# The pooling mixer of a small decoder trunk as one listed order of single steps, with the rows around the tile borders pooled by one product

## Chip, cores and metric

One core of a Trainium2 chip runs the whole program in one launch. The metric is device time in microseconds (us) of a run; three runs of the kernel before gave 982.71 (median), 980.87 and 986.82. Everything else that is read here comes from one profiled execution.

## The reference

The input `x` holds 512 rows (positions) of 1024 channels. Layer 0 mixes by pooling, layer 1 by attention, and each layer ends in an MLP. What matters here is layer 0 up to the first half of its MLP, in 32-bit floats throughout:

```python
h = rms_norm(x, mix_pre_g[0])
# group g of 256 channels, window w = 2, 4, 8, 16: mean of the last w rows (fewer at the start), minus h itself
y[:, g] = causal_mean(h[:, g], w) - h[:, g]
m = (y[:, g] @ pool_w[0, g] for each g) * pool_scale[0]
x = x + rms_norm(m, mix_post_g[0])
h = rms_norm(x, mlp_pre_g[0])
x = x + rms_norm(square(relu(h @ w_up[0])) @ w_down[0], mlp_post_g[0])
```

`rms_norm(x, g)` is `x * (mean(x*x) + 1e-6) ** -0.5 * g`.

## The kernel before

The 512 rows are four tiles of 128 rows, `xt[0]` to `xt[3]`, kept on the chip. The stage that is changed runs from the start of the program to the second halves of the first up blocks. For each tile `t`, of which every product has two halves `h` of 512 channels, it does this:

- **Square** (`q`): ScalarE sums the squares of a row. **Norm** (`x`): VectorE adds the two parts of the sum and EPS, GpSimd takes the power -0.5 (`rstd`), VectorE multiplies the tile by it into `xs[t]`.
- **Pool** (`p`): TensorE multiplies 128x128 blocks of `xs[t]` by a constant band matrix (its columns hold the weights of a mean minus the identity), and for tiles 1 to 3 adds a second product of 16 columns with the tile before, `xs[t-1]`, since a window reaches back over the border. ScalarE copies the result, which stands channels by rows, to `ys[t]`.
- **Mix** (`m`): TensorE multiplies by the group's map `wpool` (already scaled on VectorE by `linear`, step `w`, with `mix_pre_g` and with `pool_scale`, which `spread`, step `r`, has spread over all partitions by a product of a one-row matrix of ones). ScalarE sums the squares of the result, VectorE multiplies it by the gain `mix_post_g`.
- **Add** (`a`): VectorE, GpSimd and VectorE again make the factor of that norm and add to `xt[t]`; ScalarE sums the squares of the new `xt[t]`.
- **Norm and transpose** (`n`, `t`): the same three-engine chain makes the next factor, VectorE multiplies into a tile `xn`, TensorE transposes it, and ScalarE and VectorE split it into a high and a low part, `xnh` and `xnl`.

The first matrix of the MLP is worked in blocks of 128 output columns. Each block is split into high and low too (`weight`: a load, a ScalarE cast, a VectorE subtraction; step `F` does the next block) and needs three products for each of eight channel blocks. An up block has a first half, tiles 0 and 1 (256 columns), and a second half, tiles 2 and 3; `u0` to `u3` are the first halves of blocks 0 to 3, done inside the mixing stage.

Steps named `z` are warm-up products of a tile of zeros into a bank that nobody reads; there are 20. PSUM gives eight banks, taken in turn. `MIX_ORDER` lists the steps, and inside `tc.manual_schedule` each engine runs its instructions in the order in which the steps issue them. The tiles 2 and 3 that are still to be transposed at the end of the list are done by the MLP code (`pending`, `need`). Loads are issued by SyncE in the order of the code, each waiting for the one eight places before it.

After the stage the MLP (`mlp`) does the four second halves, block 4 whole, and then products of groups of blocks (line 507) that need `w_down` rows, of which one half is loaded into the buffer `xn3` of the `xn` tiles.

In `Update.rstd` the row factor of the MLP norm is taken without EPS, and `homogeneous_eps` makes up for it later with three VectorE operations of one column for each tile and layer.

Of the kernel before, what the change touches and what calls it, by code (L numbers as in the profile page):

```python
# [15 lines left out]
P = 128  # L16
D = 1024
S = 512
# [13 lines left out]
TINY = 1e-24  # L32
# [12 lines left out]
    for w in """q0 z8 r z6 q1 x0 p00 p01 z6 x1 w0 p10 p11 w1 q2 m00 x2 q3 m01 a0 m10 m11 x3 p20 p21 n0  # L45
    p30 a1 t00 t01 p31 F n1 m20 m21 F t10 t11 u0 a2 m30 F m31 u1 n2 a3 F t20 t21 u2 n3 F u3""".split()
# [11 lines left out]


# [6 lines left out]
def trunk(ctx, tc, x, consts, gcol, grow, pw, wup, wdn, wq, wk, wv, wo, out):  # L66
# [20 lines left out]
    xt = [keep.tile([P, D], F32, tag=f"x{t}", name=f"x{t}") for t in range(T)]  # L87
# [160 lines left out]
    def rstd(st, col, eps=EPS, op=ALU.add, third=False):  # L248


        total = st[:, col + 2 : col + 3]
        latest["dve"] = nc.vector.tensor_scalar(
            out=total, in0=st[:, col : col + 1], scalar1=st[:, col + 1 : col + 2],
            scalar2=eps, op0=ALU.add, op1=op,
        )
# [3 lines left out]
        latest["pool"] = nc.gpsimd.tensor_tensor(out=r, in0=total, in1=mhalf, op=ALU.pow)  # L259
        return r  # L260
# [12 lines left out]
    mlp_eps, normed_by, early = {}, {}, []  # L273

    class Update:
        def __init__(self, t, gpost, scaled, eps=EPS, gpre=None, final=False):
            self.t, self.gpost, self.scaled, self.eps = t, gpost, scaled, eps
# [12 lines left out]
        def add(self):  # L290
            r = rstd(self.st, 0, self.eps, third=len(self.cuts) > 2)
            x = xt[self.t]
            for n, cut in enumerate(self.cuts):
                latest["dve"] = nc.vector.scalar_tensor_tensor(
                    out=x[:, cut], in0=self.scaled[:, cut], scalar=r, in1=x[:, cut], op0=ALU.mult, op1=ALU.add
                )
                if self.final:
                    nc.sync.dma_start(out[TS[self.t], cut], x[:, cut])
                else:
                    square_sum(x[:, cut], self.xn[:, cut], self.st, 4 + n)  # L300

        def rstd(self):
            normed_by[self.t] = self
            if self.gpre is None:
                self.r = rstd(self.st, 4)
                return

            self.r = rstd(self.st, 4, TINY, ALU.max)  # L310

        def homogeneous_eps(self):
            m, q, r = self.st[:, 6:7], self.st[:, 0:1], self.r
            e = mlp_eps[self.t] = keep.tile([P, 1], F32, tag=f"eps{self.t}", bufs=2, name=name("eps"))
            nc.vector.tensor_scalar(out=q, in0=m, scalar1=EPS, scalar2=r, op0=ALU.add, op1=ALU.mult)
            nc.vector.tensor_scalar(out=q, in0=q, scalar1=r, scalar2=None, op0=ALU.mult)
            nc.vector.scalar_tensor_tensor(out=e, in0=q, scalar=EPS, in1=q, op0=ALU.mult, op1=ALU.mult)
# [200 lines left out]
    def mlp(l, mp, update):  # L518
# [33 lines left out]
        entering = dict(normed_by)  # L552
# [22 lines left out]
        for g, group in enumerate(groups):  # L575
# [51 lines left out]
    with tc.tile_pool(name="mix0", bufs=1, reuse_waits="tile") as mp:  # L627
# [3 lines left out]
        cst = mp.tile([P, 12 * P], F32, tag="cst", name="cst")  # L631
        band = lambda kind, g: cst[:, (kind * 4 + g) * P : (kind * 4 + g + 1) * P]
        one_row = mp.tile([1, D], F32, tag="row", name="row")
        ones = mp.tile([1, P], F32, tag="ones", name="ones")
        nc.gpsimd.memset(ones, 1.0)
        nc.sync.dma_start(cst[:, : 4 * P], consts[:, P : 5 * P])
        nc.sync.dma_start(one_row, grow[R_SCALE : R_SCALE + 1, :])
        nc.sync.dma_start(gc, gcol)
        nc.sync.dma_start(xt[1], x[TS[1], :])
        wpool = [mp.tile([P, D], F32, tag=f"pw{i}", name=f"pw{i}") for i in range(2)]  # L640
        nc.sync.dma_start(cst[:, 4 * P :], consts[:, 5 * P :])
        for i in range(2):
            nc.sync.dma_start(wpool[i], pw[i])
        gpost = gain_row(R_MIX_POST0)
        nc.sync.dma_start(xt[2], x[TS[2], :])
        nc.sync.dma_start(xt[3], x[TS[3], :])
        nc.sync.dma_start(ident, consts[:, :P])
        gpre0 = gain_row(R_MLP_PRE0, spare_tile())

        scale = mp.tile([P, D], F32, tag="scale", name="scale")  # L650
        xs, ys, ups, sts = {}, {}, {}, {}
# [6 lines left out]
        def spread():  # L658

            for n in NS:  # L660
                pr = ps()
                nc.tensor.matmul(pr, ones, one_row[:, n], start=True, stop=True)
                nc.scalar.copy(scale[:, n], pr)

        def linear(i):


            for b in range(4):
                k, g = C_MIX_PRE0 * KC + 4 * i + b, 2 * i + b // 2
                w = wpool[i][:, b * 256 : (b + 1) * 256]  # L670
                nc.vector.scalar_tensor_tensor(
                    out=w, in0=w, scalar=gc[:, k : k + 1], in1=scale[:, g * 256 : (g + 1) * 256],
                    op0=ALU.mult, op1=ALU.mult,
                )

        def squares(t):
            xs[t] = mp.tile([P, D], F32, tag=f"xs{t}", name=f"xs{t}")
            sts[t] = keep.tile([P, 8], F32, tag=f"stat{t}", bufs=4, name=name("stat"))
            if t == 0:
                for n in range(2):  # L680
                    square_sum(xt[t][:, NS[n]], xs[t][:, NS[n]], sts[t], n)
            else:
                nc.vector.memset(sts[t][:, 1:2], 0.0)
                square_sum(xt[t], xs[t], sts[t], 0)

        def scaled(t):
            r = rstd(sts[t], 0)
            for n in NS:
                nc.vector.tensor_scalar(out=xs[t][:, n], in0=xt[t][:, n], scalar1=r, scalar2=None, op0=ALU.mult)

        def pooled(t, h):
            if not h:
                ys[t] = mp.tile([P, D], F32, tag="y", bufs=2, name=f"y{t}")
            py = ps()
            for c in range(4):
                cb = 4 * h + c
                cs = slice(cb * P, (cb + 1) * P)
                nc.tensor.matmul(
                    py[:, TS[c]], xs[t][:, cs], band(0 if t == 0 else 1, cb // 2), start=True, stop=True,
                    skip_group_check=True,  # L700
                )
                if t:

                    n = max(WINDOWS)
                    nc.tensor.matmul(
                        py[:, c * P : c * P + n], xs[t - 1][:, cs], band(2, cb // 2)[:, :n], start=False,
                        stop=True, skip_group_check=True,
                    )
            nc.scalar.copy(ys[t][:, NS[h]], py)

        def mixed(t, h):
            if not h:
                ups[t] = Update(t, gpost, mp.tile([P, D], F32, tag="m", bufs=2, name=f"m{t}"), gpre=gpre0)
            pm = ps()
            for g in (2 * h, 2 * h + 1):
                o = pm[:, (g % 2) * 256 : (g % 2) * 256 + 256]
                for k in range(2):
                    cs = slice((2 * g + k) * P, (2 * g + k + 1) * P)
                    ws = slice(((g % 2) * 2 + k) * 256, ((g % 2) * 2 + k) * 256 + 256)
                    nc.tensor.matmul(o, ys[t][:, cs], wpool[h][:, ws], start=k == 0, stop=k == 1)  # L720
            ups[t].square(h, pm, nc.vector)

        def normed(t):
            ups[t].rstd()
            ups[t].norm()
            pending[t] = ups[t]

        def transposed(t, h):
            ups[t].transpose((h,))
            if h:  # L730
                pending.pop(t)

        def half_up(j):
            early.append((ps(), get(("up", 0, j))))
            up_block(*early[j], slice(0, S // 2))

        steps = {
            "q": squares, "x": scaled, "p": pooled, "m": mixed, "a": lambda t: ups[t].add(), "n": normed,
            "t": transposed, "r": spread, "w": linear, "F": fill, "z": busy, "u": half_up,
        }  # L740
        on = mybir.EngineType
        with tc.manual_schedule(engines={on.PE, on.Activation, on.DVE, on.Pool}):
            for step, which in MIX_ORDER:
                steps[step](*which)


    with tc.tile_pool(name="mlp0", bufs=1, reuse_waits="tile") as mp:
        mlp(0, mp, lambda t, y, gpost: Update(t, gpost, y, mlp_eps[t]))
# [204 lines left out]
    with tc.tile_pool(name="mlp1", bufs=1, reuse_waits="tile") as mp:  # L953
        mlp(1, mp, lambda t, y, gpost: Update(t, gpost, y, mlp_eps[t], final=True))


def constants():
# [4 lines left out]
    first, later, before = [], [], []  # L962
    for w in WINDOWS:
        inside = ((s <= t) & (s > t - w)).astype(np.float32)
        first.append(inside / np.minimum(t + 1, w).astype(np.float32) - eye)
        later.append(inside / np.float32(w) - eye)
        before.append((s - P > t - w).astype(np.float32) / np.float32(w))
    return np.concatenate([eye, *first, *later, *before], axis=1).astype(np.float32)
# [38 lines left out]
```

## Time and profile before

| | before |
|---|---|
| runs, median (lowest to highest) | 982.71 us (980.87 to 986.82) |
| profiled execution: span from first to last instruction | 984.6 us |
| TensorE (PE) busy | 959.1 us, 97% |
| VectorE (DVE) busy | 715.6 us, 73% |
| ScalarE (ACT) busy | 566.9 us, 58% |
| GpSimd (POOL) busy | 138.5 us, 14% |
| DMA | 156.88 MB, mean 159 GB/s |

The profile has no time of the profiled execution besides its span; 984.6 us is 1.9 us above the median of the runs and inside their spread. PE is the engine of the matrix products, PEld its weight loads, SPq the queue of SyncE that issues loads. A timeline row gives start and duration in us, engine, line, operation, output<-input tiles, shape and count; where the engine was idle ahead of it, brackets give how long and what ended it. Tile names are shown without their numbers.

### The profile page before, as it was taken

To read this page: it belongs to the slowest core of one execution; us is meant where nothing else is said; L and a number is where in the kernel's file an instruction comes from. 1 tells how busy PE (TensorE), PEld (TensorE's weight loads), DVE (VectorE), ACT (ScalarE), POOL (GpSimd) and SP (SyncE) were. 2 spreads that over 40 slices of the span, in tenths; PEclk is the share of its full clock that TensorE was granted. 3 is DMA by queue.
4 is the path that set the end of the run, shared out by engine and by line. 5 is a ranking of instruction groups with operands and counts; after the bars stand their busy time and mean duration, and the time that the engine had idled before them with its cause. 6 is when DMAs were issued, how large, how long until landed. Compare 5 with 4: busy or idle time off the path is not lost.

```text
span 984.6 us, 12507 instructions
## 1 busy us (share of the span) xinstructions
PE 959.1 (97%) x4804; PEld 812.2 (82%) x4804; DVE 715.6 (73%) x772; ACT 566.9 (58%) x979; POOL 138.5 (14%) x107
## 2 busy tenths in 40 slices
PE   9799999999999999999999999989999999999997
PEld 6688888878788788999799987888888888888885
DVE  3647589897897986376667688775487785957856
ACT  4537888978695556465556573446454444444532
POOL 1102030130402204100000000302031210302103
PEclk9899999999999999999999999989999999999999
DMA  6153777959678690242352423243333314133012
GB/s 249 44 192 98 265 275 227 416 199 346 243 277 326 232 342 3 89 169 86 129 214 89 168 108 121 77 145 108 128 102 112 128 56 181 29 127 122 22 43 87
DMA packets 43550, 156.88 MB, mean 159 GB/s; under 512 B 4449, under 2 KB 4833, under 8 KB 43490
## 3 DMA queue, kind: packets, MB, share of 16 engines
q1 hardware_dynamic: 43490, 156.07, 44.4%
q8 instruction: 38, 0.62, 0.2%
q14 instruction: 22, 0.18, 0.1%
HBM read 122.50 MB, written 33.55 MB: 159 GB/s over the span
## 4 chain that ended last, share of the span: by engine, by line
PE 82%; DVE 8%; ACT 4%; issue 2%; DMA 2%; POOL 1%; POOLq 0%; DVEq 0%; ACTq 0%
PE ps L507 24%; PE ps L623 13%; PE ps L624 13%; PE ps L622 13%; PE ps L264 4%; PE ps L265 4%; PE ps L263 4%; DMA xn<-in_wdn 2%; PE ps L895 2%; DVE w L130 2%; PE ps L885 1%; DVE w L243 1%; PE ps L853 1%; PE ps L854 1%; ACT xn L246 1%
## 5 line engine op out<-in xcount | busy, mean ns | idle before, releaser
L507 PE MATMUL ps<-w,a 128*128 128x512 f32 x1176 | 278.4, 389 | 2.4 <-DVE a L243 2.4
L623 PE MATMUL ps<-xnl,w 128*128 128x512 f32 (+1 forms) x712 | 263.9, 371 | 1.9 <-DVE xnl L243 1.9
L624 PE MATMUL ps<-xnh,w 128*128 128x512 f32 (+1 forms) x712 | 263.5, 370 | 0.8 <-DVE w L130 0.8
L622 PE MATMUL ps<-xnh,w 128*128 128x512 f32 (+1 forms) x712 | 263.8, 372 | 0.4 <-ACT w L128 0.4
L507 PEld LDWEIGHTS ps<-w,a 128*128 128x128 f32 x1176 | 220.5, 188 | 49.4 <-DVE a L243 3.7
L623 PEld LDWEIGHTS ps<-xnl,w 128*128 128x128 f32 x712 | 136.3, 191 | 24.3 <-DVE xnl L243 2.5
L624 PEld LDWEIGHTS ps<-xnh,w 128*128 128x128 f32 x712 | 136.2, 191 | 23.2 <-DVE w L130 1.0
L622 PEld LDWEIGHTS ps<-xnh,w 128*128 128x128 f32 x712 | 135.8, 191 | 22.8 <-ACT w L128 0.6
L130 DVE TENSOR_TENSOR w<-raw,w 128x1024 fp32r<-128x1024 f32 x66 | 83.9, 1271 | 60.2 <-ACT w L128 60.2
L128 ACT CAST w<-raw 128x1024 fp32r<-128x1024 f32 x66 | 69.0, 1047 | 84.7 <-PE ps L624 79.0
L516 DVE TENSOR_TENSOR y<-ps,y 128x512 f32<-128x512 f32 x124 | 83.2, 683 | 34.9 <-PE ps L507 34.9
L242 ACT CAST a<-r 128x768 fp32r<-128x768 f32 (+1 forms) x60 | 47.6, 793 | 65.0 <-PE ps L507 39.4
L462 POOL TENSOR_TENSOR s<-r 128x768 f32<-128x768 f32 (+1 forms) x10 | 21.7, 2172 | 373.8 <-ACT r L540 331.2
L242 ACT CAST w<-e 128x1536 fp32r<-128x1536 f32 (+1 forms) x30 | 41.9, 1398 | 54.0 <-DVE e L481 44.7
L243 DVE TENSOR_TENSOR a<-r,a 128x768 fp32r<-128x768 f32 (+1 forms) x60 | 60.0, 1003 | 14.6 <-ACT a L242 14.5
L288 POOL TENSOR_TENSOR y<-y,grow 128x512 f32<-128x512 f32 x12 | 18.7, 1556 | 314.1 <-ACT xn L246 314.1
L243 DVE TENSOR_TENSOR w<-e,w 128x1536 fp32r<-128x1536 f32 (+1 forms) x30 | 58.3, 1943 | 4.5 <-ACT w L242 4.2
L462 POOL TENSOR_TENSOR r<-r 128x768 f32<-128x768 f32 (+1 forms) x20 | 48.7, 2437 | 64.5 <-DVE a L243 49.7
L867 DVE TENSOR_TENSOR_SCAN e<-u,begin 128x1280 f32<-128x1280 f32 x16 | 45.2, 2822 | 13.3 <-ACT u L861 13.0
L139 ACT ACTIVATE apart<-apart,gc 128x128 f32<-128x128 f32 (+1 forms) x132 | 42.8, 406 | 0.0
L246 ACT ACTIVATE xn<-y 128x512 f32<-128x512 f32 (+1 forms) x25 | 15.4, 616 | 41.8 <-DVE y L369 41.8
L243 DVE TENSOR_TENSOR w<-xn,w 128x1536 fp32r<-128x1536 f32 (+1 forms) x20 | 33.0, 1651 | 5.5 <-ACT w L242 5.5
(127 smaller groups left out, 1509.9 us busy)
## 6 DMA issues: line engine op xcount, KB each, us to landing
raw<-in_wup SPq DMA_DIRECT2D x62, 512.0 KB, 3.8
w<-kept SPq DMA_DIRECT2D x58, 512.0 KB, 4.2
kept<-wx SPq DMA_DIRECT2D x30, 512.0 KB, 5.2
w<-in_wdn SPq DMA_DIRECT2D x8, 1536.0 KB, 6.4
kept<-apart SPq DMA_DIRECT2D x24, 512.0 KB, 5.1
xn<-in_wdn SPq DMA_DIRECT2D x8, 1536.0 KB, 8.3
raw<-in_wdn SPq DMA_DIRECT2D x8, 512.0 KB, 4.3
apart<-in_wk SPq DMA_DIRECT2D x7, 512.0 KB, 8.8
```

Of the source, the lines that this page charges most:

```text
L128: nc.scalar.copy(hi, raw)
L130: nc.vector.tensor_tensor(out=lo, in0=raw, in1=hi.bitcast(F32), op=ALU.subtract)
L139: nc.scalar.mul(c, c, gc[:, lo + k : lo + k + 1])
L242: latest["act"] = nc.scalar.copy(hi, src)
L243: latest["dve"] = nc.vector.tensor_tensor(out=lo, in0=src, in1=hi.bitcast(F32), op=ALU.subtract)
L462: sub = lambda out, x, y, op=ALU.subtract: nc.gpsimd.tensor_tensor(out=out, in0=x, in1=y, op=op)
L507: nc.tensor.matmul(bank, a[:, x, q, TS[t]], w[:, z, q], start=start and q == 0 and k == 0, stop=q == self.n - 1 and k == 2, skip_group_che ...
L516: nc.vector.tensor_tensor(out=part, in0=bank, in1=part, op=ALU.add)
L622: nc.tensor.matmul(pu[:, cols], wh[:, k, :], xnh[:, k, cols], start=k == 0, stop=False)
L623: nc.tensor.matmul(pu[:, cols], wh[:, k, :], xnl[:, k, cols], start=False, stop=False)
L624: nc.tensor.matmul(pu[:, cols], wl[:, k, :], xnh[:, k, cols], start=False, stop=k == KC - 1)
L867: nc.vector.tensor_tensor_scan(out=e[:, ::-1], data0=u[:, 1:][:, ::-1], data1=begin[:, ::-1], initial=0.0, op0=ALU.mult, op1=ALU.max,)
```

## The change

The mixing stage becomes one list of 135 single steps, each of one engine (`h` issues its load too), and the list takes in what was left to the MLP code and to `fill`: all transposes, the splits of up weights 0 to 3 (`h`, `l`) and the four first halves (`U`).

- **The row norm moves into the band.** `x` isn't scaled any more. The sum of squares goes straight to GpSimd's power (the tiles are two columns wider, and the extra column holds the value whose square stands for EPS), and VectorE multiplies the constant band (`b`) by the row factor.
- **The borders are pooled by one product.** The 30 rows around each of the three borders are loaded once more into a tile `edge` (90 rows), and one set of products of 46 columns gives the 15 rows behind each border. The tiles 1 to 3 then need products of 114 columns for their other 113 rows, and none with the tile before.
- `spread` has matrices of 128 rows, all but one zero, in place of one row. Nine warm-up products are left of 20: eight ahead and one behind the two spreads. The loads stand in another order: the maps and the edge rows come ahead of `xt[1]`.
- The pooled rows of all tiles go to one tile `yt`. The additions to `xt` are one instruction of 1024 columns in place of two of 512, and so are the squares of the new `xt`.
- EPS is added in every norm, and `homogeneous_eps` with its 24 VectorE instructions is gone.

The core of the diff:

```diff
-    for w in """q0 z8 r z6 q1 x0 p00 p01 z6 x1 w0 p10 p11 w1 q2 m00 x2 q3 m01 a0 m10 m11 x3 p20 p21 n0
-    p30 a1 t00 t01 p31 F n1 m20 m21 F t10 t11 u0 a2 m30 F m31 u1 n2 a3 F t20 t21 u2 n3 F u3""".split()
+    for w in """z8 S0 q0 C0 S1 r0 b0 z1 P00 L00 L02 C1 c00 P01 L03 q4 L01 L13 r4 L10 L11 c01 L12 M00 M01 b4 q1 r1 b1 s00
...
-            self.r = rstd(self.st, 4, TINY, ALU.max)
-
-        def homogeneous_eps(self):
-            m, q, r = self.st[:, 6:7], self.st[:, 0:1], self.r
...
-            else:
-                with tc.issue_after(latest["dve"].ins):
-                    while entering:
-                        entering.popitem()[1].homogeneous_eps()
...
+        edge = mp.tile([3 * EDGE, D + 2], F32, tag="edge", name="edge")
+        windows = {**dict(enumerate(xt)), T: edge}
+        for w in windows.values():
+            nc.vector.memset(w[:, D:], (EPS * D) ** 0.5)
...
         for i in range(2):
             nc.sync.dma_start(wpool[i], pw[i])
+        for i in range(3):
+            lo = (i + 1) * P - EDGE // 2
+            nc.sync.dma_start(edge[i * EDGE : (i + 1) * EDGE, :D], x[lo : lo + EDGE, :])
+        nc.sync.dma_start(xt[1][:, :D], x[TS[1], :])
...
+        def mean_square(t, col):
+            r = rows(t)
+            nc.scalar.activation(
+                junk[r, : D + 1], windows[t][:, : D + 1], ACT.Square, scale=D**-0.5,
+                accum_out=sts[t][r, col : col + 1],
+            )
...
+        def power(t, col):
+            r = rows(t)
+            nc.gpsimd.tensor_tensor(
+                out=sts[t][r, col + 1 : col + 2], in0=sts[t][r, col : col + 1], in1=mhalf[r], op=ALU.pow
+            )
+
+        def scaled_band(t):
+            kind, r = 0 if t == 0 else 2 if t == T else 1, rows(t)
+            n = 4 * BANDS[kind]
+            band[t] = mp.tile([P, 4 * P], F32, tag="band", bufs=3, name=f"band{t}")
+            nc.vector.tensor_scalar(
+                out=band[t][r, :n], in0=bands[r, starts[kind] : starts[kind] + n], scalar1=sts[t][r, 1:2],
+                scalar2=None, op0=ALU.mult,
+            )
+
+        def pooled(t, h):
+            py = pys[t, h] = ps()
+            n, r = BANDS[0 if t == 0 else 2 if t == T else 1], rows(t)
+            at = BORDER if t == T else P
+            for i, c in enumerate(range(KC) if t == T else range(4 * h, 4 * h + 4)):
+                nc.tensor.matmul(
+                    py[:, i * at : i * at + n], windows[t][r, c * P : (c + 1) * P],
+                    band[t][r, c // 2 * n : c // 2 * n + n], start=True, stop=True, skip_group_check=True,
                 )
-                if t:
-
-                    n = max(WINDOWS)
-                    nc.tensor.matmul(
-                        py[:, c * P : c * P + n], xs[t - 1][:, cs], band(2, cb // 2)[:, :n], start=False,
-                        stop=True, skip_group_check=True,
-                    )
...
+        steps = {
+            "q": squares, "r": lambda t: power(t, 0), "b": scaled_band, "P": pooled, "c": pooled_out,
+            "S": spread, "C": spread_out, "L": linear, "M": mixed, "s": mixed_square, "g": mixed_gain,
+            "e": total, "E": lambda t: power(t, 4), "A": added, "w": lambda t: mean_square(t, 6),
+            "v": lambda t: power(t, 6), "N": normed, "T": transposed, "H": high, "X": low,
+            "h": weight_high, "l": weight_low, "U": half_up, "z": busy,
+        }
```

A step's digits are its tile and half (`T20`: tile 2, first half; tile 4 is `edge`), or its block (`U3`, `h3`, `l3`).

What the lists make of the engines' queues is seen in two places. On TensorE, where tile 2 is pooled out and the up blocks begin, the kernel before has this (L698 and L705 pool, L720 mixes, L334 transposes, L622 to L624 are the up block):

```order
L698 MATMUL ps25_306<-cst_88,xs3_213 128x128
L705 MATMUL ps25_306<-cst_88,xs2_196 128x16
L720 MATMUL ps29_327<-pw0_96,y2_250 128x256 x4
L720 MATMUL ps30_334<-pw1_97,y2_250 128x256 x4
L334 MATMUL ps33_346<-ident_74,xn3_80 128x128 x4
L334 MATMUL ps34_353<-ident_74,xn3_80 128x128 x4
L622 MATMUL ps35_360<-xnh_81,w26_316 128x256
```

and the changed one this (L708 pools, L731 mixes, L765 transposes, L607 to L609 are the up block):

```order
L765 MATMUL ps32_287<-ident_74,xn3_80 128x128 x4
L731 MATMUL ps33_292<-pw0_99,yt_120 128x256 x4
L731 MATMUL ps34_297<-pw1_100,yt_120 128x256 x4
L731 MATMUL ps35_308<-pw0_99,yt_120 128x256 x4
L765 MATMUL ps36_315<-ident_74,xn3_80 128x128 x4
L708 MATMUL ps38_322<-band2_206,x2_72 128x114 x4
L765 MATMUL ps39_329<-ident_74,xn3_80 128x128 x4
L731 MATMUL ps40_336<-pw1_100,yt_120 128x256 x4
L607 MATMUL ps41_348<-xnh_81,w23_247 128x256
```

Before, the first up block stands right behind the transposes of tile 1, with the mixes of tile 3 behind it; now all mixes stand ahead of the up blocks, and between the two transposes of tile 1 (ps36, ps39) stands a pooling product that doesn't need them.

On VectorE, the kernel before has this around the splits of tile 1 (L243 splits, L252 is the one-column sum ahead of GpSimd's power, L294 adds to `xt`, L288 applies the gain, L130 splits a weight, L325 norms):

```order
L130 TENSOR_TENSOR w31_341<-raw32_342,w31_341 128x1024
L243 TENSOR_TENSOR xnl_82<-ps33_346,xnh_81 128x4x128
L243 TENSOR_TENSOR xnl_82<-ps34_353,xnh_81 128x4x128
L252 TENSOR_SCALAR stat28_326<-stat28_326 128x1
L294 SCALAR_TENSOR_TENSOR x2_72<-m2_325,stat28_326,x2_72 128x512 x2
L288 TENSOR_TENSOR m3_391<-ps37_393,grow1_101 128x512
```

and the changed one this (L756 norms, L739 gain, L777 splits, L743 sum, L749 adds):

```order
L756 SCALAR_TENSOR_TENSOR xn3_80<-x1_71,stat12_179,spare2_116 128x512 x2
L739 TENSOR_TENSOR m37_320<-ps34_297,grow1_112 128x512
L777 TENSOR_TENSOR xnl_82<-ps32_287,xnh_81 128x4x128
L777 TENSOR_TENSOR xnl_82<-ps36_315,xnh_81 128x4x128
L777 TENSOR_TENSOR xnl_82<-ps39_329,xnh_81 128x4x128
L743 TENSOR_SCALAR stat17_214<-stat17_214 128x1
L739 TENSOR_TENSOR m37_320<-ps33_292,grow1_112 128x512
L749 SCALAR_TENSOR_TENSOR x3_73<-m37_320,stat17_214,x3_73 128x1024
```

The split of an up weight no longer stands right ahead of the splits of tile 1, and tile 3 is worked ahead of tile 2.

More of the change, by code (lines that the diff above doesn't have):

```diff
@@ L44 @@
     (w[0], [int(c) for c in w[1:]])
-    for w in """q0 z8 r z6 q1 x0 p00 p01 z6 x1 w0 p10 p11 w1 q2 m00 x2 q3 m01 a0 m10 m11 x3 p20 p21 n0
-    p30 a1 t00 t01 p31 F n1 m20 m21 F t10 t11 u0 a2 m30 F m31 u1 n2 a3 F t20 t21 u2 n3 F u3""".split()
+    for w in """z8 S0 q0 C0 S1 r0 b0 z1 P00 L00 L02 C1 c00 P01 L03 q4 L01 L13 r4 L10 L11 c01 L12 M00 M01 b4 q1 r1 b1 s00
+    q2 s01 g00 e0 r2 P40 c40 g01 E0 b2 A0 P10 q3 c10 P11 r3 w0 P20 b3 v0 c11 M10 N00 P30 N01 h0 M11 T00 P31
+    l0 s10 h1 c30 g10 s11 l1 c20 e1 g11 H00 E1 A1 X00 c31 h2 T01 M30 M31 w1 v1 l2 s30 N10 s31 M20 H01 N11 T10
+    g31 P21 X01 H10 T11 c21 H11 M21 s21 X10 X11 e3 s20 g30 E3 U0 A3 w3 g21 e2 g20 h3 E2 A2 w2 v3 U1 N30 N31
+    v2 l3 N21 T30 H30 U2 T21 T31 H31 N20 H21 T20 X30 X31 H20 X21 X20 U3""".split()
 ]
@@ L630, in trunk @@
         nc.gpsimd.memset(warm, 0.0)
[L631 to L634, printed above, removed]
+        row = mp.tile([P, D], F32, tag="row", name="row")
+        nc.vector.memset(row, 0.0)
+        ones = mp.tile([P, P], F32, tag="ones", name="ones")
         nc.gpsimd.memset(ones, 1.0)
-        nc.sync.dma_start(cst[:, : 4 * P], consts[:, P : 5 * P])
@@ L652, in trunk @@
+        yt = mp.tile([P, KC, S], F32, tag="yt", name="yt")
+        sts, band, pys, pms, ms, xns, pts, pus = {}, {}, {}, {}, {}, {}, {}, {}
         pwarm = ps()
@@ L676, in squares @@
[L676 to L689, printed above, removed]
@@ L961, in constants @@
     eye = (s == t).astype(np.float32)
-    first, later, before = [], [], []
+    first, rest, border = [], [], []
     for w in WINDOWS:
```

179 lines of the change are left out of this document (109 added, 70 removed).

## The prediction

> **What bounds the kernel now.** I read the page first: how long, and by what.
>
> ```profile
> span 984.6 us, 12507 instructions
> ...
> PE 82%; DVE 8%; ACT 4%; issue 2%; DMA 2%; POOL 1%; POOLq 0%; DVEq 0%; ACTq 0%
> ```
>
> TensorE makes 82% of the chain that ended last. The rest must stand somewhere, so I cut the start by the view of windows (columns: window, its length, PE busy, weight loads, DVE, ACT, POOL, granted clock, DMA share, GB/s). The chain of waits puts the first second half of an up block at 66.99 and the first product of line 507 at 84.47; the other cuts are where the clock changes.
>
> ```profile
> 1.31:66.99 65.68, 58.18 (x329) 46.73 (x329) 33.26 (x65) 29.09 (x64) 6.69 (x13) 0.95 0.43 158
> 43.35:50.17 6.82, 5.45 (x24) 5.41 (x25) 3.45 (x6) 1.39 (x4) 0.55 (x1) 0.50 0.26 80
> 50.17:66.99 16.82, 15.02 (x105) 13.25 (x103) 9.57 (x16) 6.19 (x13) 1.65 (x3) 1.00 0.54 187
> 66.99:84.47 17.48, 17.48 (x121) 16.33 (x122) 11.38 (x11) 10.21 (x15) 0.68 (x1) 1.00 0.47 155
> 84.47:130.00 45.53, 45.53 (x203) 37.70 (x202) 28.11 (x28) 36.76 (x64) 6.82 (x6) 1.00 0.63 217
> ```
>
> From 66.99 on PE has no gap: 17.48 of 17.48 and 45.53 of 45.53. So whatever makes PE reach that point earlier shifts the rest with it. In the changed stage PE is idle for 65.68 - 58.18 = 7.5 us, and runs a spell of 6.82 us at half the clock. Who it waits for:
>
> ```profile
> PE ps L334 <- DVE xn L325: 2.8, 2, 2.2
> PE ps L623 <- DVE xnl L243: 1.9, 1, 1.9
> PE ps L698 <- DVE xs L689: 1.4, 1, 1.4
> ```
>
> These 6.1 of the 7.5 us are VectorE's results arriving late: norm, split and scaling, in a queue where each stands behind another tile's work.
>
> **The prices.** From the timeline, the step from one row's start to the next:
>
> ```profile
> 1.31 3.60 PE L656 MATMUL ps<-warm 128*128 128x512 bf16 x8 [1.31 <-POOL warm L630]
> ...
> 4.29 0.63 ACT L246 ACTIVATE xs<-x 128x512 f32<-128x512 f32 x1
> ...
> 4.84 3.78 PE L662 MATMUL ps<-row,ones 1*128 1x512 f32 x4
> 8.55 2.74 PE L656 MATMUL ps<-warm 128*128 128x512 bf16 x6
> 11.09 2.69 PE L698 MATMUL ps<-cst,xs 128*128 128x128 f32 x16
> 13.61 1.46 PE L656 MATMUL ps<-warm 128*128 128x512 bf16 x6
> ...
> 15.27 0.47 PE L698 MATMUL ps<-cst,xs 128*128 128x128 f32 x2
> 15.57 0.29 PE L705 MATMUL ps<-cst,xs 128*128 128x16 f32 x2
> 15.71 0.47 PE L698 MATMUL ps<-cst,xs 128*128 128x128 f32 x2
> ...
> 18.39 7.15 PE L720 MATMUL ps<-pw,y 128*128 128x256 f32 x32
> 25.38 0.39 PE L698 MATMUL ps<-cst,xs 128*128 128x128 f32 x2
> ...
> 32.31 1.33 PE L334 MATMUL ps<-ident,xn 128*128 128x128 f32 x8
> 33.48 0.39 PE L698 MATMUL ps<-cst,xs 128*128 128x128 f32 x2
> ...
> 45.53 0.41 PE L623 MATMUL ps<-xnl,w 128*128 128x256 f32 x1
> 45.74 0.41 PE L624 MATMUL ps<-xnh,w 128*128 128x256 f32 x1
> ...
> 56.07 0.28 PE L623 MATMUL ps<-xnl,w 128*128 128x256 f32 x1
> 56.19 0.28 PE L624 MATMUL ps<-xnh,w 128*128 128x256 f32 x1
> ```
>
> - Warm-up product: (11.09 - 8.55)/6 = 0.42 us early, about 0.22 us in the row of 13.61. So the clock was half until some point behind 11.09 and full before 13.61.
> - Both spreads: 8.55 - 4.84 = 3.71.
> - Pooling: a block of 128 columns with its border product is four rows, 15.71 - 15.27 = 0.44; 0.11 a row, whether of 128 columns or of 16. A half tile of four blocks: 1.76 with borders, 0.88 without. (Two rows are one 32-bit product.)
> - A mix: (25.38 - 18.39)/32 x 8 = 1.75. A half tile's transposes: (33.48 - 32.31)/2 = 0.58.
> - A first half of an up block is 24 products: at 0.12 each 2.88; in the half-clock spell at 0.21 it is 5.1, so that spell cost block 0 about 2.2.
>
> Products of 46 and 114 columns don't occur before. Below, 0.11 a row times 46/128 is 0.04; above, 0.11. I take 0.11, since 16 columns cost as much as 128 there. P40 is then 16 x 0.11 = 1.76, or 0.64 at the least.
>
> **PE's sum.** Before, work at these prices: warm-ups 14 x 0.42 + 6 x 0.22 = 7.2, spreads 3.7, pooling of tile 0 2.5 (11.09 to 13.61), of the others 6 x 1.76 = 10.6, mixes 14.0, transposes 4.7, up halves 11.5 + 2.2. That is 56.4 of 65.68, so 9.3 are waits with their filling and draining. After: nine warm-ups 8 x 0.42 + 0.22 = 3.6, spreads 3.7, pooling 8 x 0.88 + 1.76 = 8.8, mixes 14.0, transposes 4.7, up halves 11.5: 46.3. With 0.2 for the row that the spreads read, PE would be through at 1.31 + 46.5 = 47.8 if it never waited.
>
> **What PE waits for after.** I walked the four listed queues with the durations of these groups (mean ns), ends of one engine to starts of the next 0.05 us apart.
>
> ```profile
> L246 ACT ACTIVATE xs<-x 128x1024 f32<-128x1024 f32 x3 | 3.2, 1056 | 0.0
> L246 ACT ACTIVATE xn<-ps 128x512 f32<-128x512 f32 x8 | 4.8, 597 | 4.0 <-PE ps L720 3.8
> L259 POOL TENSOR_TENSOR stat<-stat,mhalf 128x1 f32<-128x1 f32 x12 | 6.6, 551 | 56.8 <-DVE stat L252 56.8
> L689 DVE TENSOR_SCALAR xs<-x,stat 128x512 f32<-128x512 f32 x8 | 3.5, 484 | 2.7 <-POOL stat L259 2.7
> L325 DVE SCALAR_TENSOR_TENSOR xn<-x,stat,spare 128x512 f32<-128x512 f32 x8 | 5.7, 748 | 2.7 <-POOL stat L259 2.7
> L243 DVE TENSOR_TENSOR xnl<-ps,xnh 128x512 fp32r<-128x512 f32 x7 | 4.5, 684 | 2.1 <-ACT xnh L242 2.1
> L130 DVE TENSOR_TENSOR w<-raw,w 128x1024 fp32r<-128x1024 f32 x4 | 4.9, 1222 | 2.7 <-ACT w L128 2.7
> L683 DVE MEMSET stat<- 128x1 f32 x3 | 0.2, 59 | 0.0
> ```
>
> - Tile 0, whose second half is there by 4.29: square to 5.5, power 0.55, band 0.48: ready at 6.6, while PE is with the spreads until 8.6. Hidden.
> - M10 needs c10. ScalarE from c00 at 10.0: c00, q4, c01, q1, s00, q2, s01 end at 15.9, edge copies behind P40 (16.1) at about 17.0, q3 at 18.1, c10 at 18.6; PE gets there at 18.6. A tie.
> - T10 needs N10: A1 ends at 26.8, w1 on ScalarE waits behind h2, whose load leaves when l0 frees its buffer (23.0, load 3.7), so w1 ends at 28.9, power 29.5, N10 30.3. PE comes at 30.1: waits 0.2.
> - U0 needs X11 at 33.8, PE comes at 34.3. U1 to U3 need weights split 4 us earlier. The last splits (X20) end at 47.2, PE is free at 47.8.
>
> So PE waits little by the walk, but everywhere with slack below 1 us; I allow 0.9, and put the second halves at **48.7**. Gain 66.99 - 48.7 = **18.3**: warm-ups 3.6, pooling 4.3, half-clock spell 2.2, waits 8.2. The fewer and wider instructions on DVE and ACT pay only through those waits. The 24 operations of `homogeneous_eps` stand where PE has no gap, and cost or bring nothing.
>
> Where the stall goes, the loads come next. One half of `w_down` goes into `xn` and leaves only when the last transpose is done; VectorE works on it before the first product of line 507:
>
> ```profile
> 67.01 0.38 SPq L446 DMA_DIRECT2D xn<-in_wdn  x1
> ...
> 74.77 1.23 DVE L481 TENSOR_TENSOR e<-xn,w 128x1024 f32<-128x1024 f32 x1 [4.95 <-DMA xn<-in_wdn]
> ...
> 83.21 0.69 DVE L243 TENSOR_TENSOR a<-r,a 128x512 fp32r<-128x512 f32 x1 [0.28 <-ACT a L242]
> ```
>
> DVE ends at 83.90 and PE starts at 84.47: 0.6 us of slack. After, T20 stands ahead of U3, so this load leaves 2.9 us earlier against PE: slack 3.5. Early loads: maps and edge rows have 2.1 MB ahead of and with them where the second map had 2.8 MB and landed by about 10.3 (issued at 4.3, 6.0 in the view of DMAs):
>
> ```profile
> 3.83 0.91 SPq L643 DMA_DIRECT2D pw<-in_pw  x2
> ...
> pw<-in_pw SPq DMA_DIRECT2D x2, 512.0 KB, 6.0
> ```
>
> So the edge rows land by 9, and q4 wants them at 10.5. The memset of 128x1024 on DVE, for which the load of the one row waits, isn't shown: between 0.06 (one column) and 1.2 (a DVE operation of 128x1024). I take nothing, since three loads are issued ahead of it; at 1.2 the spreads would start up to 0.4 later.
>
> **The clock.** It is the largest unknown. The rows show it half until past 11.09 although PE had no real gap from 1.31. I put it at full from 8.6, between two bounds: full only at 12.6 would make 3.8 us of pooling and mixing run at half, and by the walk the end moves to 51.5; full from 5.8 makes it 46.9.
>
> [...]
>
> **The rivals.**
> - *A half-clock spell inside the new stage.* The old one began after PE had idled 2.2 us at the transposes and again 1.9 us. [...] Against: by the walk no wait over 0.3 us. Price: 6.82 us at half is 3.4 lost: 967.9. [...]
> - *ScalarE or VectorE becomes the bound.* The squares of the norms all write one tile and wait for each other, and slack is under 1 us. If 20 hand-overs cost 0.3 us more, 6 us of the gain go: about 970, to 975 at twice that.
> - *The gain is given back at line 507*, if the `w_down` load takes over 11.2 us (7.7 + 3.5). At 14 us it is 967. Against: 7.7 in the trace.
> - *Slower*: the clock stays half through the whole stage, on pooling and transposes too thin to lift it. Then 39.0 us of work behind the spreads take 78: +39 - 18 = 21 slower, 1003. It decides from 18.3 us of work at half clock lost, just under half of the stage. Against: before, the same kinds of product held 1.00 for 30 us.
> - *Nothing visible*: SyncE's in-order queue holds the weight loads for the old places, so that U0 to U3 stand at the old times. The walk shows the buffers free at 23 and 25, so hardly: 980.
>
> **How the numbers follow.** 984.6 - 18.3 = 966.3 for the profiled execution; the runs' median lies 1.9 below its span, so **964.4**. Chances: forecast (ends 46 to 51.5) 0.74, half-clock spell 0.10, other engines bound 0.09, given back 0.02, nothing 0.02, slower 0.03. Bounds: the walk's 46.9 less 1.1 for a cheap P40 gives 45.8, gain 21.2, 961.5; 51.5 and a spell give 971. Runs spread by 3 us on either side, in part by two more half-clock spells (10 us) later on. Range 959 to 973. A change of 1% (9.8 us) is about what a measurement tells from none: faster by that 0.91, within 0.06, slower 0.03.
>
> **What would show it.** Second halves at 48 to 49, no PE wait over 0.5 us between 9 and 48, idle under 2 us in all; pooling rows of 46 and 114 columns 0.11 apart; the row of 507 some 17.5 us behind the second halves, with PE at 100% in between. It is wrong if PE's waits name ScalarE's copies (M10, M20), if the clock reads 0.50 in the stage, or if DVE's wait for `xn` ends behind PE's arrival at line 507.

## The result, and the profile after

| | before | after |
|---|---|---|
| runs beside each other, median (lowest to highest) | 984.77 us (980.87 to 988.32) | 972.68 us (971.76 to 974.25) |
| ratio, 95% interval | | 0.989 (0.9855 to 0.9924) |
| profiled execution, span | 984.6 us | 970.0 us |
| second halves of the up blocks begin | 66.99 us | 48.80 us |

The kernel is faster by 12 us, not by the 18 that the forecast of 964.4 meant; the time lies at the upper end of the range (959 to 973). Yet the stage gained what was forecast: 18.2 us between the two profiled executions. The rest of the page shows no new engine in the chain:

```profile
span 970.0 us, 12402 instructions
...
PE 92%; DVE 3%; ACT 2%; issue 1%; DMA 1%; SPq 0%; POOL 0%; DVEq 0%; POOLq 0%; ACTq 0%
```

The view of windows, cut at the second halves (48.80) and 17.52 us behind them, as the prediction cut the kernel before at 66.99 and 84.47 (the first product of line 507 starts at 84.31 there; the same line, 497 now, starts at 65.78). The column of the granted clock counts nothing ahead of the first rise on record, here at 5.37:

```profile
1.31:48.80 47.49, 44.39 (x285) 37.99 (x286) 31.94 (x56) 30.77 (x61) 9.09 (x14) 1.00 0.67 231
48.80:66.32 17.52, 17.52 (x125) 16.39 (x124) 10.29 (x10) 9.86 (x15) 3.72 (x3) 1.00 0.44 156
66.32:112.00 45.68, 45.68 (x200) 37.16 (x199) 27.49 (x28) 35.79 (x63) 3.52 (x4) 1.00 0.60 207
```

PE idles 3.1 us in the stage (47.49 - 44.39) where it idled 7.5 (forecast: under 2), and has no gap behind it, as forecast. But the last row hides the loss: 200 products recorded in 45.68 us, where before had 203 in 45.53. A busy engine may be busy with dearer instructions. The groups of products by line and shape show which (columns: count, busy us, mean ns of one, idle). Before:

```profile
L507 PE MATMUL ps<-w,a 128*128 128x512 f32 x1176 | 278.4, 389 | 2.4 <-DVE a L243 2.4
L622 PE MATMUL ps<-xnh,w 128*128 128x512 f32 x568 | 221.3, 390 | 0.0
L624 PE MATMUL ps<-xnh,w 128*128 128x512 f32 x568 | 221.1, 389 | 0.0
L623 PE MATMUL ps<-xnl,w 128*128 128x512 f32 x568 | 221.1, 389 | 0.0
```

After:

```profile
L497 PE MATMUL ps<-w,a 128*128 128x512 f32 x1176 | 278.8, 390 | 0.0
L609 PE MATMUL ps<-xnh,w 128*128 128x512 f32 x568 | 224.5, 395 | 0.0
L607 PE MATMUL ps<-xnh,w 128*128 128x512 f32 x568 | 224.4, 395 | 0.0
L608 PE MATMUL ps<-xnl,w 128*128 128x512 f32 x568 | 224.2, 395 | 0.0
```

Each of the 1704 up products with 512 columns takes 5 to 6 ns longer; their rows add up to 673.1 us against 663.5. Their code is the same. The timeline shows it in one block, 24 products and the first of the next line. After:

```profile
101.82 0.40 PE L607 MATMUL ps<-xnh,w 128*128 128x512 f32 x1
102.06 0.39 PE L608 MATMUL ps<-xnl,w 128*128 128x512 f32 x1
102.28 0.40 PE L609 MATMUL ps<-xnh,w 128*128 128x512 f32 x1
102.52 0.39 PE L607 MATMUL ps<-xnh,w 128*128 128x512 f32 x1
...
107.42 0.63 PE L497 MATMUL ps<-w,a 128*128 128x512 f32 x2
```

Before:

```profile
119.67 0.39 PE L622 MATMUL ps<-xnh,w 128*128 128x512 f32 x1
...
125.11 0.61 PE L507 MATMUL ps<-w,a 128*128 128x512 f32 x2
```

(107.42 - 101.82)/24 = 233.3 ns from start to start; (125.11 - 119.67)/24 = 226.7. Over the whole traces, waits and half-clock spells left out, this **step** of the up products is 233.0 ns against 227.0, and 6.0 x 1704 = 10.2 us is what the stage's gain lost on the way to the end.

What changed for them is where their operands lie. In these products `xnh` or `xnl` streams in 512 columns past a block of `w` that TensorE has loaded. The change makes each of the four `xt` two columns wider. In the compiled programs' memory maps `xnh` starts at 17408 before (68 x 256) and at 17536 after (68 x 256 + 128), 32 bytes further for each `xt`, while `w` starts at a multiple of 256 in both. The maps are no view of the profile; what follows rests on runs whose gaps are known to the byte.

### The profile page after: what moved, and what is told of

It reads as the page before. It is cut to its first block, busy times and chain, and to the rows that moved or that the text cites. A ratio compares the mean times of both kernels' runs of the same rounds, so it can differ in the third digit from the quotient of the medians.

```text
span 970.0 us, 12402 instructions
## 1 busy us (share of the span) xinstructions
PE 951.6 (98%) x4761; PEld 801.0 (83%) x4761; DVE 709.8 (73%) x736; ACT 568.7 (59%) x974; POOL 144.2 (15%) x108
## 4 chain that ended last, share of the span: by engine, by line
PE 92%; DVE 3%; ACT 2%; issue 1%; DMA 1%; SPq 0%; POOL 0%; DVEq 0%; POOLq 0%; ACTq 0%
PE ps L497 28%; PE ps L609 15%; PE ps L607 15%; PE ps L608 15%; PE ps L268 4%; PE ps L269 4%; PE ps L267 4%; PE ps L957 2%; PE ps L947 1%; PE ps L731 1%; DVE e L929 1%; PE ps L915 1%; PE ps L916 1%; DMA edge<-in_x 1%; PE ps L708 1%
## 5 line engine op out<-in xcount | busy, mean ns | idle before, releaser
L609 PE MATMUL ps<-xnh,w 128*128 128x512 f32 (+1 forms) x712 | 265.1, 373 | 0.0
L607 PE MATMUL ps<-xnh,w 128*128 128x512 f32 (+1 forms) x712 | 265.0, 373 | 0.0
L608 PEld LDWEIGHTS ps<-xnl,w 128*128 128x128 f32 x712 | 134.3, 189 | 25.2 <-DVE xnl L247 0.3
L609 PEld LDWEIGHTS ps<-xnh,w 128*128 128x128 f32 x712 | 134.1, 188 | 25.4
L607 PEld LDWEIGHTS ps<-xnh,w 128*128 128x128 f32 x712 | 134.0, 189 | 24.4
L132 ACT CAST w<-raw 128x1024 fp32r<-128x1024 f32 x62 | 65.0, 1049 | 87.8 <-PE ps L609 83.4
L452 POOL TENSOR_TENSOR r<-r 128x768 f32<-128x768 f32 (+1 forms) x20 | 52.2, 2608 | 59.3 <-DVE a L247 58.5
L247 DVE TENSOR_TENSOR w<-e,w 128x1536 fp32r<-128x1536 f32 (+1 forms) x30 | 55.9, 1862 | 3.1 <-ACT w L246 2.7
```

Source lines behind the costliest of these rows:

```text
L132: nc.scalar.copy(hi, raw)
L247: latest["dve"] = nc.vector.tensor_tensor(out=lo, in0=src, in1=hi.bitcast(F32), op=ALU.subtract)
L452: sub = lambda out, x, y, op=ALU.subtract: nc.gpsimd.tensor_tensor(out=out, in0=x, in1=y, op=op)
L607: nc.tensor.matmul(pu[:, cols], wh[:, k, :], xnh[:, k, cols], start=k == 0, stop=False)
L608: nc.tensor.matmul(pu[:, cols], wh[:, k, :], xnl[:, k, cols], start=False, stop=False)
L609: nc.tensor.matmul(pu[:, cols], wl[:, k, :], xnh[:, k, cols], start=False, stop=k == KC - 1)
```

## The experiments

### Which start decides

The theory was the start address of the streamed tiles; the rival, that the new stage disturbs what runs behind it (loads, VectorE). The edits only leave gaps beside `xnh` and `xnl`:

```diff
+    keep.tile([P, 32], F32, tag="ahead", name="ahead")      # 128 bytes
     xnh = keep.tile([P, KC, S], F32R, tag="xnh", name="xnh")
     xnl = keep.tile([P, KC, S], F32R, tag="xnl", name="xnl")
+    keep.tile([P, 32], F32, tag="behind", name="behind")    # 128 bytes
```

A name gives the kernel (a: changed, b: before) and the bytes left free ahead of `xnh` and behind `xnl`.

**a_128_128.** 

> Changed kernel with 128 bytes a partition left free ahead of xnh (start 17536 to 17664, a multiple of 256 again) and 128 behind xnl, so that everything behind keeps its start modulo 256. Theory (start address): products of up blocks on xnh and xnl go back from 233 to 227 ns a row, some 1690 products x 6 ns = 10 us less than the changed kernel's 972.7, so 961 to 965. Rival (the new stage disturbs what runs behind it, by loads or by VectorE): pitch stays at 233, time 970 to 975.

**b_128_128.** 

> Kernel before with the same two gaps: only xnh and xnl move by 128 modulo 256 (17408 to 17536). Theory (start address): its up products slow from 227 to 233 ns and the time rises by 8 to 11 us, with the stage unchanged. Rival (something in the new stage): pitch 227, time within 2 us of before.

**b_0_128.** 

> Kernel before with 128 bytes left free behind xnl alone: xnh and xnl keep their start, all tiles behind (w, a, dn, sq and the rest) move by 128 modulo 256. If the start of the operand that streams counts, up products stay at 227 ns, and those of line 507, where w streams, go from 227 to about 233: 1176 x 6 ns = 7 us more. If the start of the loaded 128x128 operand counts as well, the up products slow down too: 17 us more. If neither (xnh and xnl only): no change.

**b_256_0.** 

> Kernel before with 256 bytes left free ahead of xnh: everything moves by 256. Theory (start modulo 256): pitch stays at 227 and the time that of before. If it is the start modulo 512 or 1024 that counts, or where tiles lie against each other: pitch of up products about 233, 8 to 10 us more.

**a_0_128.** 

> Changed kernel with 128 bytes left free behind xnl alone: xnh and xnl stay at 128 modulo 256 (17536), and w and everything behind moves to 128 modulo 256 too. If the difference between the starts of the streamed and the loaded tile counts (modulo 256): up products 227 ns, time 962 to 966. If every tile must start at a multiple of 256: 233 ns or more, time 972 and above.

**b_64_192.** 

> Kernel before with xnh and xnl moved by 64 against everything else (64 bytes free ahead, 192 behind). If any difference modulo 256 costs: up products about 230 to 236 ns, as those of ohl (64 modulo 256, 236 ns), 5 to 15 us more than before. If only a half of 256 costs: 227 ns, no change.

**b_32_224.** 

> Kernel before with xnh and xnl moved by 32 against everything else (32 free ahead, 224 behind). If any difference modulo 256 costs: 230 to 236 ns; if it must be a multiple of 64 or more to cost: 227 ns.

Step is the mean from start to start of the up products of 512 columns in the profiled execution, without waits and half-clock spells; the starts are those of `xnh` and of `w`, modulo 256. The runs were made on several chips, on which the kernel before had 982.89 to 984.77; a ratio is to the kernel before on the same chip.

| kernel | xnh | w | step, ns | time, us |
|---|---|---|---|---|
| before | 0 | 0 | 227.0 | 984.77 |
| after | 128 | 0 | 233.0 | 972.68 |
| a_128_128 | 0 | 0 | 227.0 | 964.27 (961.56 to 966.91), ratio to before 0.9807 (0.9776 to 0.9838) |
| b_128_128 | 128 | 0 | 233.0 | 993.24 (992.11 to 995.42), ratio to before 1.0106 (1.0077 to 1.0135) |
| b_256_0 | 0 | 0 | 227.0 | 985.29, one run |
| b_0_128 | 0 | 128 | 233.0 | 988.46, one run |
| a_0_128 | 128 | 128 | 227.1 | 963.89, one run |
| b_64_192 | 64 | 0 | 229.7 | 988.22, one run |
| b_32_224 | 32 | 0 | 233.5 | 995.87, one run |

The groups' rows say the same, first of `a_128_128` and of `b_128_128`, where only `xnh` and `xnl` moved:

```profile
L609 PE MATMUL ps<-xnh,w 128*128 128x512 f32 x568 | 221.3, 390 | 0.0
```

```profile
L626 PE MATMUL ps<-xnh,w 128*128 128x512 f32 x568 | 224.3, 395 | 0.0
```

Then of `b_0_128`, where only `w` and what lies behind moved, and of `a_0_128`, where `w` moved by as much as `xnh` had:

```profile
L625 PE MATMUL ps<-xnh,w 128*128 128x512 f32 x568 | 224.3, 395 | 0.0
```

```profile
L608 PE MATMUL ps<-xnh,w 128*128 128x512 f32 x568 | 221.3, 390 | 0.0
```

The rival falls with `b_128_128`: the old stage with 128 bytes of gap is 1.1% slower. My first form of the theory (the streamed tile must start at a multiple of 256) falls with `b_0_128`, and is corrected by `a_0_128`: what counts is the **difference** between the starts of the streamed and the loaded tile. At 0 modulo 256 the step is 227 ns; at 32, 64 and 128 it is 2.7 to 6.5 ns more. `a_128_128` is the changed kernel without the accident, and stands where the forecast stood.

### Other products

**a_a128.** Tile `a`, loaded in line 507's products, behind a gap of 128 bytes (beside `a_gaps_2`, which is `a_128_128` again, as the base on the same chip).

> The changed kernel with both gaps of 128 bytes, as in a_128_128, as the base for the run beside it on one chip: 962 to 966.

> As a_gaps_2, but the tile a, which is loaded as the 128x128 operand in line 507's products, starts 128 bytes later, against w, which streams. If the difference of starts counts in every product of this kind: those 1176 go from 227 to about 233 ns, 7 us more than a_gaps_2, and the up products stay at 227. Rival (it concerns xnh and xnl only): 227 everywhere, no change.

966.42 us (965.21 to 969.16) against 964.65 (963.69 to 967.34). The expectation was wrong in its setting: the streamed `w` of these products is a tile of the same pool, behind `a`, and moved with it. So their difference stayed at 0 and their step nearly so, 227.0 to 227.6 ns; the rise is in the first product of each row of them, which follows an up product (226.6 to 230.9), and in the last, which an up product follows (226.6 to 232.4). The tile `dn`, mostly moved as well, streams past `sq`, which wasn't: that step rose from 227.8 to 232.2 ns over 180 products. The two times overlap in their spread, so the steps decide, not the time. The groups of `a_gaps_2` and of `a_a128`:

```profile
L267 PE MATMUL ps<-dn,sq 128*128 128x512 f32 x60 | 23.5, 392 | 0.0
```

```profile
L267 PE MATMUL ps<-dn,sq 128*128 128x512 f32 x60 | 23.7, 396 | 0.0
```

**a_c01_att** puts 192 bytes behind the attention's tile `u1`, so that `ohl` starts at a multiple of 256 and not 64 behind one, and lists `c01` ahead of `q4`:

```diff
-    c00 P01 L03 q4 L01 L13 r4 L10 L11 c01 L12 M00 M01
+    c00 P01 L03 c01 q4 L01 L13 r4 L10 L11 L12 M00 M01
...
         us = [ap.tile([P, NSEG + 1], F32, tag=f"u{a}", name=f"u{a}") for a in range(2)]
+        ap.tile([P, 48], F32, tag="gap", name="gap")
```

> Changed kernel with both gaps of 128 bytes, the step c01 listed ahead of q4, and 192 bytes left free behind u1, so that v, q, k, ohl start at multiples of 256. Order: M01 no longer stands behind the square of the edge rows; it can start when the second map's rows are scaled (12.9 in the run a_128_128 against 14.55), and the edge product follows it: the 3.1 us wait falls to about 1.5 and the second halves start 1.0 to 1.6 us earlier. Rival: the wait moves to the edge product, no gain. Gap: the 168 products of w and ohl go from 236 to 227 ns, 1.6 us less; rival: they stay at 236. Both: 960 to 963, against 964.3.

962.90 us (961.37 to 964.88), ratio to before 0.9799 (0.9766 to 0.9832). Leaving out waits and half-clock spells, the mean step of the products with `ohl` fell from 232.9 ns (`a_gaps_2`; 8 of 136 steps at 228 or less) to 228.6 (101 of 142). So the rule holds here too, but it is worth 4.3 x 168 = 0.7 us, half of what was expected, and too little to see in the time.

### The wait that is left in the stage

PE's waits in the stage of the changed kernel, and the timeline rows behind them:

```profile
PE ps L731 <- ACT yt L723: 2.8, 2, 2.6
PE ps L731 <- DVE pw L667: 0.3, 1, 0.3
```

```profile
4.90 2.18 PE L658 MATMUL ps<-row,ones 128*128 128x512 f32 x4
6.92 0.38 PE L654 MATMUL ps<-warm 128*128 128x512 bf16 x1
7.13 1.95 PE L708 MATMUL ps<-band,x 128*128 128x128 f32 x16
...
14.04 1.99 PE L731 MATMUL ps<-pw,yt 128*128 128x256 f32 x8 [2.62 <-ACT yt L723]
15.87 1.88 PE L708 MATMUL ps<-band,edge 90*128 90x46 f32 x16
17.57 2.91 PE L708 MATMUL ps<-band,x 128*128 128x114 f32 x24
20.32 1.90 PE L731 MATMUL ps<-pw,yt 128*128 128x256 f32 x8
```

```profile
12.37 1.06 ACT L679 ACTIVATE junk<-edge 90x1025 f32<-90x1025 f32 x1 [3.56 <-DMA edge<-in_x]
```

M01 (14.04) needs the copy `c01`, and `c01` stands behind `q4` in ScalarE's queue, which waits 3.56 us for the edge rows. Listing `c01` first lets it go:

> The same with the step c01 listed ahead of q4, and nothing else. If the wait of M01 is what the order costs: the second halves start 1.0 to 1.6 us earlier than in a_gaps_2 and the median falls by as much. Rival (the chip's loads decide, whatever the order): within 0.5 us of a_gaps_2.

963.36 us (963.31 to 963.89) on the chip on which `a_gaps_2` had 964.65 (963.69 to 967.34), and the second halves at 47.73 against 48.77. PE's waits there, `a_gaps_2` first:

```profile
PE ps L733 <- ACT yt L725: 3.0, 2, 2.9
```

```profile
PE ps L710 <- DVE band L700: 0.6, 2, 0.4
PE ps L733 <- DVE pw L669: 0.3, 1, 0.3
PE ps L733 <- ACT yt L725: 0.2, 1, 0.2
```

PE's idle time in the stage falls by 1.9 us, and 1.0 arrives at the second halves. The wait for `yt` is 2.1 to 3.4 us in all five executions with 128 rows and the old order, and 0.2 in both with the new one, so that the order ends it is shown; what it is worth at the second halves is not, since they began between 47.71 (`a_0_128`) and 49.32 (`a_128_128`) with the old order too. `a_c01` (0.9789 of before, 0.976 to 0.9817) and `a_c01_att` are the fastest versions; between the two nothing is told apart.

### What the prediction had at nothing, and the clock

**b_noeps** takes `homogeneous_eps` out of the kernel before and adds EPS in every norm, as the change does.

> Kernel before without homogeneous_eps, EPS added in every norm as in the changed kernel; all tiles keep their start modulo 256. Theory (its operations delay VectorE's queue): the three waits for a fall from 3.2 us to 1 to 2, and the time by 1 to 2.5 us. Rival (as the prediction had it, it costs nothing): waits of about 3 us, time within 1 us of before.

981.58 us (980.03 to 984.54) against 984.52, ratio 0.9979 (0.9963 to 0.9995): small, but not nothing. PE's waits between 190 and 345 us, before and in `b_noeps`:

```profile
PE ps L507 <- DVE a L243: 2.4, 3, 0.9
```

```profile
PE ps L501 <- DVE a L243: 1.1, 2, 0.7
```

From start to start 3.2 us are lost before and 1.7 in `b_noeps`, where the first of the three waits, at 205 us, is gone. The likely way: the first twelve of these VectorE operations stand between 142 and 151 us, in a queue that is busy for 55.3 of the 60 us from 130 to 190, and what they delay reaches PE some 60 us later.

**The spreads and the clock.** These go with two single runs of the changed kernel (gaps of 128) with spreads of one row, and one of before with spreads of 128. The changes of the granted clock on record lie whole multiples of 3.41 us apart: before at 12.63, 43.35, 50.18, 599.72, 603.13, 650.92, 657.75 and 982.02, which are 9, 2, 161, 1, 14, 2 and 95 times 3.413 apart, and after at 5.37, 633.42, 636.83 and 967.93 (184, 1 and 97). Such a stretch is what an expectation here calls a window of the clock.

> As a_gaps_2, but the two spreads multiply one row of ones with the one row, as before, not 128 rows. If products of one row don't lift the clock: it rises at 12 to 14 us, as before, and the second halves start some 2 to 3 us later. If they have nothing to do with it: it rises at 5 to 8 us.

> A second look at a_onerow. If products of one row don't hold the clock up: again a half-clock spell that begins between 5 and 12 us, and second halves 1.5 to 3 us behind 48.8. If that was the phase of the clock's windows alone: full from 5 to 8 us on, and 48.8.

> Kernel before with the two spreads by matrices of 128 rows, all but one zero, in place of one row. If products of one row don't hold the clock up: it rises at 5 to 8 us, as in the changed kernel, and the second halves start 2 to 4 us earlier than 67. If the spreads have nothing to do with it: it rises at 12 to 14 us.

With 128 rows the granted clock rose between 4.9 and 7.4 us in all eight executions, and was not lost again before 27.7. With one row it rose at 12.6 to 13.9 in six of nine (`a_onerow_2`: 13.48), at 5.1 and 5.3 in two (`b_noeps`, `b_0_128`), and in `a_onerow` at 4.49, to be halved twice more:

```profile
4.49:7.90 3.41, 3.26 (x13) 1.58 (x13) 0.49 (x1) 2.32 (x4) 0.55 (x1) 1.00 1.00 335
7.90:11.31 3.41, 3.41 (x16) 3.14 (x15) 1.67 (x5) 0.58 (x1) 0.00 (x0) 0.50 1.03 205
11.31:14.73 3.42, 1.27 (x7) 0.79 (x5) 1.67 (x4) 1.74 (x4) 0.51 (x1) 1.00 1.03 384
14.73:18.14 3.41, 3.41 (x8) 2.77 (x9) 1.46 (x3) 2.77 (x6) 1.09 (x3) 0.50 1.03 413
```

In the changed kernel the second halves then began at 51.12 and 49.46, against 47.7 to 49.3 with 128 rows; in `b_rows128` at 64.96, 2.0 earlier than before, but two executions of its stage with one row and an early rise had 63.3 (`b_noeps`) and 63.4 (`b_0_128`). The times, single runs, are 965.70 (`a_onerow`), 965.05 (`a_onerow_2`) and 982.61 (`b_rows128`), all within the spread of their base. The stretches of 3.41 us ahead of the two half-clock spells are the first and the third row: the third has 1.27 us of products, and in the first 1.95 of 3.26 us are the one-row spreads. So a rise behind 12 us, or a clock lost again by 20, was seen in seven of nine executions with one row and in none of eight with 128. That products of one row count for too little to hold the clock is the author's estimate from these counts. Why the other two with one row rose early was not shown: where the stretches fall against the spreads wasn't set in any run.

## Why the prediction was off, step by step

- **The failed step** is "So whatever makes PE reach that point earlier shifts the rest with it". It rested on PE having no gap, and took for granted that the products behind keep their price. Two more columns in four tiles moved `xnh` by 128 bytes, and 1704 products took 6.0 ns more. The missing term is +10.2 us for the up products, and +0.5 for the first ones of line 497 (1176 products, 227.1 to 227.5). The trace of before had a hint: the products with `ohl`, of the same shape but 64 bytes off, stepped at 232.9 ns there and all others at 227.
- **No gap from 66.99 on** was read only as far as 130. At 205, 267 and 328 us PE waited for VectorE's `a`, and lost 3.2 us from start to start; in the changed kernel it lost nothing there. About half of that is `homogeneous_eps`, forecast to "cost or bring nothing"; the slower up products, which give VectorE more time, hide the rest (with the step back at 227 ns, the changed kernel with 128-row spreads loses 1.0 to 2.1 us there; `b_128_128`, the kernel before with the slow step, loses nothing).
- **Half-clock spells behind the stage** were put into the range, not into the sum. Before had 10.24 us of them in the profiled execution, after 3.41; at half the work in such a spell (the granted clock reads 0.50, and the products with `ohl` step 427 ns in the one at 599.72, against 232.9 outside), that is an estimated 3.4 us in favour. As far as the runs show that is chance: other executions have 3.4 to 10.2 us of them with the old stage, and 3.4 to 6.8 with the new one. Before:

```profile
599.72:603.13 3.41, 3.41 (x8) 2.76 (x9) 2.45 (x5) 0.00 (x0) 0.00 (x0) 0.50 0.50 154
650.92:657.75 6.83, 6.06 (x29) 6.09 (x30) 3.90 (x5) 2.12 (x3) 0.00 (x0) 0.50 0.44 137
```

  After:

```profile
633.42:636.83 3.41, 2.83 (x14) 2.86 (x15) 2.02 (x4) 1.44 (x3) 0.00 (x0) 0.50 0.00 0
```

  The sum is now -18.2 - 3.2 - 3.4 + 10.2 + 0.5 = -14.1, against 970.0 - 984.6 = -14.6. That is between the profiled executions; the medians differ by 12.1. The prediction took 1.9 us off the span to get the median. After the change the run that was profiled took 971.85 for its span of 970.0, 1.85 more, and the median was 972.68; with as much on top of 984.6, the profiled execution before stood near 986.4, above the medians of 982.71 and 984.77. So 2.5 us of the 14.6 belong to these two executions.
- **The stage, 48.7, came out at 48.80**, but that was luck: two errors cancel. The clock was full from 5.37, not 8.6: the four spread products took 2.0 us (4.90 to 6.92), not 3.7. And PE waited 3.1 us, not 0.9 and 0.2, of it 2.6 at once for a copy of ScalarE, where no wait over 0.5 was to be; it was M01, not M10 or M20. The edge rows were to land by 9 and landed at 12.2. The estimate went by bytes: about 1 MB less is ahead of the second map than before. But the map landed at 10.18 (before 10.64), issued at 3.35 (before 4.30), and the three loads of 30 rows behind it took 7.2 us each at the median (columns: count, size of one, us from issue to landing):

```profile
edge<-in_x SPq DMA_DIRECT2D x3, 120.0 KB, 7.2
```

  Other executions of the same order put the second halves at 47.7 to 49.3 with 128-row spreads, and the kernel before and its variants at 63.3 to 68.1, so one pair of executions gives the gain of 18.2 to no better than some 2 us.
- **Right:** the eight warm-ups ahead of the spreads take 3.59 (1.31 to 4.90), forecast 3.4. A pooling product of 46 columns takes (17.57 - 15.87)/16 = 0.106 us and one of 114 (20.32 - 17.57)/24 = 0.115, forecast 0.11. Tile 0's pooling takes 1.79, forecast 1.76. The half-clock spell of block 0 is gone, no such spell fell into the stage, and M10 and T10 didn't wait. Line 497 starts 17.0 us behind the second halves (48.80 to 65.78; before 17.3) with PE full, so the load for it gave nothing back.
- **The rivals:** none of them was it. 970 to 975, the time of "ScalarE or VectorE becomes the bound", came by another road.
- **Small slips of the sums**, none of which decides: 964.4 + 3.4 is 967.8, not 967.9, and a loss of 12 us gives 976, not 975. A rise of the clock at 12.6 or 5.8 in place of 8.6, at half the work in the time between, moves the end to 50.7 or 47.3; 51.5 and 46.9 come from a walk that isn't shown. Before rose at 12.63; no run shows 5.8, which was a choice, and the early rises on record came at 4.49 to 7.4. Line 507's first product starts at 84.31, so the slack there was 0.4 us, not 0.6.

## What to carry to other kernels

When a change alters the size of any tile in a pool that lives through the whole kernel, compare the starts of all tiles behind it, modulo 256, before and after, and those of the two operands of each frequent product with each other; a gap of 128 bytes ahead of `xnh` and one behind `xnl` were worth 8.4 us here (972.68 to 964.27), nearly half of what the whole rewritten stage brought. Behind a stage, compare the price of one frequent instruction, not only the idle time: an engine at 100% can still be slower. In a queue with listed order, what depends on a load goes behind what doesn't.

## What the hardware showed that was not expected

- A 32-bit product in the form used here (128x128 loaded, 512 columns streamed) steps at 227.0 ns when both tiles start at the same address modulo 256, at 229.7 with 64 between them, and at 233.0 and 233.5 with 128 and 32. With 128 the steps alternate, 237 or 238 and 229 or 230 ns. The difference alone doesn't fix the price: in the products with `ohl`, where it is the loaded tile that lies 64 further, the step is 232.9. What makes the difference is not settled. Line 497's first products behind an up block are slow after the change too (230 to 233 ns for three, then 227), though their own tiles lie 0 apart. And in `a_a128`, where the two tiles of each up product and of each product of that line lie 0 apart and only the two kinds differ, by 128, the last product ahead of each change of kind and the first behind it take 230.8 to 232.5 ns, and the others 227. That would fit a cost of what is loaded for the next product while the last tile still streams (from 48.80 to 66.32 in the changed kernel PEld is busy for 16.39 us and PE for all 17.52), but no run separates the two.
- First up halves, with 256 columns streamed, show no such loss: 120 ns in the most frequent step in before and after.
- While the three loads of 30 rows (120 KB each) were under way, between 8 and 10 us, 209 and 274 KB a microsecond came in; in the same two microseconds before it had been 418 and 406. That the small loads cause this wasn't tried.
